# Stick-breaking attention in a hybrid decoder step: when the room of a pair's sample and meta key rows goes back to the arena

## The chip, the cores and the metric

The kernel runs on one core of one Trainium2 chip. The metric is the device time of one execution in microseconds (us); three timed runs of the kernel before gave 1514.38, 1515.96 and 1517.47 us, median 1515.96 us. One more execution was recorded by the profiler; every row of a trace below is from it.

The engines of a core are PE (matrix products, with PEld for its weight loads), DVE (elementwise work and scans), ACT (activations and copies), POOL (masks, memsets and gathers) and SP, which here only issues transfers. Each engine takes its instructions strictly in program order, and waits on counters (semaphores) that the other engines and the transfers raise.

## The reference

One layer of a decoder, with 512 prompt tokens behind 16 meta tokens, and 8 running sequences of 4 new tokens each with 256 cached positions. D_MODEL is 1024, and the attention has 16 heads of 64.

```python
def layer(x, s0, past_k, past_v, lead, ...):
    h = x + 0.5 * rms_norm(swiglu(rms_norm(x, ffn1_pre_g), ...), ffn1_post_g)
    proj = rms_norm(h, mix_pre_g) @ w_in
    q_a, k_a, v_a, gk_low, r_a, q_b, k_b, v_b, gate_a, gate_b = jnp.split(proj, offs, axis=-1)
    o_a, s_new = gla_branch(...)                      # gated linear attention, in chunks
    keys, vals = k_b, v_b                             # or the cached pages with k_b, v_b behind them
    o_b = sb_attend(q_b, keys, vals, sb_bias, q_off)  # stick-breaking attention
    m = sigmoid(gate_a) * (o_a @ w_o_gla) + sigmoid(gate_b) * (o_b @ w_o_sb)
    h = h + rms_norm(m @ w_out, mix_post_g)
    y = h + 0.5 * rms_norm(swiglu(rms_norm(h, ffn2_pre_g), ...), ffn2_post_g)
    return y, k_b, v_b, s_new

# sb_attend, for a query t and keys s < t:  z = q.k / 8 + bias
# A[t, s] = sigmoid(z_ts) * prod over s < j < t of (1 - sigmoid(z_tj))
```

The outputs that the change touches are the new key rows: `k_sample` (32 rows of the samples, output 5) and the first 16 rows of `k_prompt` (the meta tokens, output 2).

## The kernel before

The program is written out in order: PE, DVE, ACT and POOL execute what the code records, in the order in which it records it (`manual_schedule`). The main loops feed PE with matrix products of 128x128 weights in high and low halves (`tile_steps`, lines 681 to 684), and after each eighth of such a product, a **half step**, one call of `step()` runs the side work that has come due. `later(n, f)` puts a piece of side work n half steps ahead; `then(n, f)` puts it at half step n of the present pair.

**The attention** goes over 16 heads as 8 pairs, `Pair(0)` to `Pair(7)`, in a loop of nine passes of 24 half steps each. In a pass PE makes the queries, keys and values of the present pair (in the ninth pass, which has none, three gates instead) and the side work finishes the pair of the pass before. Of that side work these matter here:

- half step 6, `tails` (line 1735): PE transposes the pair's last 48 key columns (32 sample and 16 meta tokens; L1739), DVE copies them to `tk`, a room of 128 columns (L1745), and two transfers on SP's queue bring `tk` to the outputs: 16 KB of sample rows (L1747) and 8 KB of meta rows (L1748). Then `give(tk)`.
- half steps 9 to 14, `turned` (line 1755): three blocks of attention weights for each of the two heads are transposed by PE (L1763) and copied out of PSUM to a room `t` of 512 columns (L1766), by ACT for the first head and by DVE for the second.
- half step 14, `meta_turned` (PE L1788), and half step 17, `summed` (PE L1779, products with the values).

The passes of pairs 4 to 7 also work on the samples' cached pages: POOL issues gathers of 256 KB each (L1825), PE transposes the pages (L1874) and ACT copies them out. In the last pass these are eight gathers in a row.

**Rooms.** SBUF is one arena of 150 units of 280 columns in 25 chunks, `room0` to `room24`. `take(width)` finds units that are free in the recorded order, and prefers those that have been free for longest (`since`), after rules on evenness and on chunks still empty; `give` marks them free. Neither is an instruction. A room that is taken after it was given gets its new writer made to wait for what still reads or writes it, by waits that the framework adds. So `give` tells when a room may be found again, and a wait follows for whoever finds it while its old readers, here two transfers, have not ended. PSUM has two such rings of four buffers, `ps` and `acc`, that turn in the order of use.

Where the order of instructions is printed below, `room16_41_5215` is a chunk of the arena, `ps731` a PSUM buffer, and `DMAHW7_49` one of the eight counters on which SP's transfers are counted in turn; a transfer waits for the one before it on its own counter, so the names in SP's own rows tell on which it is counted.

Of the kernel before, what the change touches and what calls it, by code (L numbers as in the profile page):

```python
# [44 lines left out]
MIXER += [("S", "a", 4), ("R", "p", 2), ("R", "p", 3), ("S", "b", 4), ("S", "a", 6), ("R", "p", 4), ("R", "p", 5), ("S", "b", 6)]  # L45
MIXER += [("R", "p", 6), ("R", "p", 7)]
AHEAD = 150
SPREAD = 15
UNITS = 150


class Arena:
# [13 lines left out]
    def take(self, width, dt=F32, tight=False):  # L66
        k = -(-width // self.UNIT)
        best = None
        empties = sum(None not in f for f in self.freed)
        for c, free in enumerate(self.freed):  # L70
            empty = None not in free
            if not empty and self.tile[c].dtype != dt:
                continue
            for s in range(self.CHUNK - k + 1):
                f = free[s : s + k]
                if None in f:
                    continue
                since = max(f) if not empty else max(free) + SPREAD
                waste = k % 2 == 0 and s % 2
                alone = k == 1 and free[s ^ 1] is not None  # L80
                key = (empty and empties <= self.keep, waste, tight and sum(x is not None for x in free), alone, since)
                if best is None or key < best[0]:
                    best = (key, c, s)
        assert best is not None, f"no room for {width}: {[sum(x is not None for x in f) for f in self.freed]}"
        _, c, s = best
        if None not in self.freed[c] and (self.tile[c] is None or self.tile[c].dtype != dt):
            self.made += 1
            self.tile[c] = self.pool.tile([P, self.CHUNK * self.UNIT], dt, tag=f"room{c}", name=f"room{c}_{self.made}")
        self.freed[c][s : s + k] = [None] * k
        a = self.tile[c][:, s * self.UNIT : s * self.UNIT + width]  # L90
        self.held[id(a)] = (a, c, s, k)
        return a
# [9 lines left out]
    def give(self, *aps):  # L102
        for a in aps:
            _, c, s, k = self.held.pop(id(a))
            self.clock += 1
            self.freed[c][s : s + k] = [self.clock] * k
# [14 lines left out]
def hybrid_step(  # L121
# [16 lines left out]
    take, give = arena.take, arena.give  # L138
# [8 lines left out]
    def ps(tag="ps"):  # L147
        count[0] += 1
        return pp.tile([P, 512], F32, tag=tag, name=f"{tag}{count[0]}")
# [566 lines left out]
    def later(n, f):  # L716
        todo.append([n, f])
# [884 lines left out]
    class Pair:  # L1602
# [133 lines left out]
        def tails(self):  # L1736
            pr, kf, vf = self.pr, self.kf, self.vf
            p = ps()
            T.transpose(p[:NTL, :P], kf[:, :NTL], ident)  # L1739
            T.transpose(p[:NTL, P : 2 * P], vf[:, NP:], ident)  # L1740
            T.transpose(p[:, 2 * P : 3 * P], vfm[pr % 2], ident)
            fc = slice(P * (pr % 4), P * (pr % 4) + P)
            self.vm = vm = take(P)
            tk = take(P)
            V.tensor_copy(tk[:NTL], p[:NTL, :P])  # L1745
            c = slice(self.c0, self.c0 + P)
            nc.sync.dma_start(k_sample.rearrange("o b t h d -> (o b t) (h d)")[:, c], tk[:NS])  # L1747
            nc.sync.dma_start(kp_out[:NM, c], tk[NS:NTL])  # L1748
            give(tk)
            V.tensor_copy(tail_v[pr // 4][:NTL, fc], p[:NTL, P : 2 * P])  # L1750
            V.tensor_copy(vm, p[:, 2 * P : 3 * P])
            give(kf, vf)
# [700 lines left out]
```

## Time and profile before

| what | us |
|---|---|
| median of three timed runs | 1515.96 |
| the profiled execution, its own time | 1509.63 |
| span of its records | 1507.9 |
| PE busy in the span | 1495.4 (99%) |
| DVE busy | 1038.6 (69%) |
| ACT busy | 758.5 (50%) |
| POOL busy | 149.1 (10%) |

The span is the time from the first to the last record of the execution; 1.7 us of its own time lie around it. Busy times are sums over instructions; an engine that is busy 99% of the span is one for which nearly all the others' waits cost nothing, and only its own idle stretches can be taken out. The chain of waits is the work that ended last, followed back from the end; the table of waits says who stood still until whom. In a timeline row stand start, duration, engine, line, operation and the number of instructions merged; in brackets the idle time before the first of them and what ended it.

### The profile page before, as it was taken

What the parts mean: (1) busy time and instruction counts of PE and PEld (TensorE: products, weight loads), DVE (VectorE), ACT (ScalarE), POOL (GpSimd) and SP (SyncE); (2) the same over time, 40 slices, a digit from 0 to 9 for tenths busy, and PEclk for the clock granted to TensorE, in tenths of its full rate; (3) what the DMA queues carried; (4) which work ended last, traced back from release to release, by engine and by line L of the source; (5) the groups of instructions that cost most, each with busy time, mean ns of one, the idle gap of its engine ahead of it and who ended that gap; (6) DMA issues with size and microseconds to landing.
All of it is one profiled execution on the core that took longest, in us unless ns stands there. A gap on an engine that the chain in (4) does not pass through costs nothing.

```text
span 1507.9 us, 29580 instructions
## 1 busy us (share of the span) xinstructions
PE 1495.4 (99%) x11959; PEld 1444.0 (96%) x11959; DVE 1038.6 (69%) x1831; ACT 758.5 (50%) x1400; POOL 149.1 (10%) x216
## 2 busy tenths in 40 slices
PE   9999999999999999999999999999999999999998
PEld 8999999999999889899988999999999999999997
DVE  5888888523787857777776534977567888885234
ACT  6445454433665657565555443534564554544234
POOL 2000000000000111123224651000000000000000
PEclk9999999999999999999999999999999999999999
DMA  8123334524655473334455668434531343334343
GB/s 250 55 86 99 98 98 137 145 77 131 161 138 154 124 108 84 92 83 119 126 105 131 189 195 194 110 96 136 168 111 50 101 145 110 99 97 118 90 116 99
DMA packets 279561, 181.84 MB, mean 121 GB/s; under 512 B 10154, under 2 KB 264416, under 8 KB 279424
## 3 DMA queue, kind: packets, MB, share of 16 engines
q1 hardware_dynamic: 273968, 163.09, 41.0%
q0 software_dynamic: 5440, 16.85, 3.1%
q8 instruction: 94, 1.54, 0.4%
q14 instruction: 43, 0.35, 0.1%
q10 hardware_dynamic: 16, 0.00, 0.0%
HBM read 157.17 MB, written 22.74 MB: 119 GB/s over the span
## 4 chain that ended last, share of the span: by engine, by line
PE 95%; DVE 2%; DMA 1%; ACT 1%; issue 0%; SPq 0%; DVEq 0%; ACTq 0%
PE acc L694 10%; PE acc L697 10%; PE acc L695 10%; PE acc L681 8%; PE acc L1146 8%; PE acc L1144 8%; PE acc L1145 8%; PE acc L682 7%; PE acc L684 7%; PE acc L1087 2%; PE acc L1084 2%; PE acc L1085 2%; PE ps L1779 1%; PE acc L924 1%; PE acc L925 1%; PE acc L926 1%
## 5 line engine op out<-in xcount | busy, mean ns | idle before, releaser
L152 DVE TENSOR_TENSOR lo<-raw,hi 128x1024 fp32r<-128x1024 f32 (+1 forms) x216 | 258.6, 1198 | 174.8 <-ACT hi L660 166.3
L152 DVE TENSOR_TENSOR room<-room,room 128x544 fp32r<-128x544 f32 (+16 forms) x367 | 237.4, 669 | 122.4 <-ACT room L738 55.7
L681 PE MATMUL acc<-room,hi 128*128 128x280 f32 (+1 forms) x928 | 271.4, 309 | 0.1
L1146 PE MATMUL acc<-room,lo 128*128 128x280 f32 (+1 forms) x896 | 259.5, 290 | 0.0
L1145 PE MATMUL acc<-room,hi 128*128 128x280 f32 (+1 forms) x896 | 259.3, 289 | 0.0
L1144 PE MATMUL acc<-room,hi 128*128 128x280 f32 (+1 forms) x896 | 259.1, 289 | 0.0
L682 PE MATMUL acc<-room,hi 128*128 128x280 f32 (+1 forms) x928 | 250.5, 289 | 0.0
L694 PE MATMUL acc<-room,hi 128*128 128x280 f32 (+1 forms) x784 | 222.0, 292 | 0.0
L695 PE MATMUL acc<-room,hi 128*128 128x280 f32 (+1 forms) x784 | 219.0, 290 | 0.0
L660 ACT CAST hi<-raw 128x1024 fp32r<-128x1024 f32 (+1 forms) x130 | 131.9, 1015 | 145.0 <-PE acc L695 125.3
L684 PE MATMUL acc<-room,lo 128*128 128x280 f32 (+1 forms) x928 | 192.8, 289 | 0.0
L697 PE MATMUL acc<-room,lo 128*128 128x280 f32 (+1 forms) x784 | 192.3, 290 | 0.0
L681 PEld LDWEIGHTS acc<-room,hi 128*128 128x128 f32 x928 | 174.9, 188 | 13.0 <-issue 11.0
L682 PEld LDWEIGHTS acc<-room,hi 128*128 128x128 f32 x928 | 175.1, 189 | 2.8 <-issue 1.9
L1146 PEld LDWEIGHTS acc<-room,lo 128*128 128x128 f32 x896 | 168.6, 188 | 0.0
L1144 PEld LDWEIGHTS acc<-room,hi 128*128 128x128 f32 x896 | 168.6, 188 | 0.0
L1145 PEld LDWEIGHTS acc<-room,hi 128*128 128x128 f32 x896 | 168.4, 188 | 0.0
L694 PEld LDWEIGHTS acc<-room,hi 128*128 128x128 f32 x784 | 147.6, 188 | 2.0 <-issue 0.9
L695 PEld LDWEIGHTS acc<-room,hi 128*128 128x128 f32 x784 | 147.6, 188 | 0.2
L684 PEld LDWEIGHTS acc<-room,lo 128*128 128x128 f32 x928 | 145.0, 188 | 0.0
L855 ACT CAST hi<-raw 128x1024 fp32r<-128x1024 f32 x86 | 90.1, 1052 | 107.8 <-PE acc L1145 47.0
L697 PEld LDWEIGHTS acc<-room,lo 128*128 128x128 f32 x784 | 134.0, 188 | 0.0
(352 smaller groups left out, 2858.2 us busy)
## 6 DMA issues: line engine op xcount, KB each, us to landing
raw<-in_w_in_dram SPq DMA_DIRECT2D x49, 512.0 KB, 7.2
raw<-in_ffn_w_down_dram SPq DMA_DIRECT2D x42, 448.0 KB, 3.9
raw<-in_ffn_w_gate_dram SPq DMA_DIRECT2D x64, 256.0 KB, 3.3
raw<-in_ffn_w_up_dram SPq DMA_DIRECT2D x64, 256.0 KB, 3.3
raw<-in_ffn_w_down_dram SPq DMA_DIRECT2D x21, 512.0 KB, 4.0
out_dram<-room SPq DMA_DIRECT2D x32, 256.0 KB, 3.1
raw<-in_w_in_dram SPq DMA_DIRECT2D x28, 256.0 KB, 4.3
h_dram<-room SPq DMA_DIRECT2D x24, 280.0 KB, 3.1
```

What stands on the lines that cost most here:

```text
L152: (eng or V).tensor_tensor(out=out, in0=a, in1=b, op=op)
L660: S.copy(h_, src)
L681: T.matmul(acc[h][:, : wid[h]], hi[k], a[h][0], start=(k == 0), stop=False)
L682: T.matmul(acc[h][:, : wid[h]], hi[k], a[h][1], start=False, stop=False)
L684: T.matmul(acc[h][:, : wid[h]], lo[k], a[h][0], start=False, stop=(k == KD - 1))
L694: T.matmul(acc[h][:nw, : wid[h]], wh, a[h][0], start=(k == 0), stop=False)
L695: T.matmul(acc[h][:nw, : wid[h]], wh, a[h][1], start=False, stop=False)
L697: T.matmul(acc[h][:nw, : wid[h]], wl, a[h][0], start=False, stop=(k == kt - 1))
L855: S.copy(hi[:, :kt], src)
L1144: T.matmul(x[:, :QW], hi, act[k][0], start=(first and k == 0), stop=False, skip_group_check=True)
L1145: T.matmul(x[:, :QW], hi, act[k][1], start=False, stop=False, skip_group_check=True)
L1146: T.matmul(x[:, :QW], lo, act[k][0], start=False, stop=(k == 3), skip_group_check=True)
```

## The change

In `tails`, the room `tk` is no longer given back in the half step that issues its two transfers, but by `later(LEAVE, ...)` twelve half steps later, at half step 18 of the pass instead of 6.

```diff
 AHEAD = 150
+LEAVE = 12
 SPREAD = 15
@@ class Pair, tails
             nc.sync.dma_start(k_sample.rearrange("o b t h d -> (o b t) (h d)")[:, c], tk[:NS])
             nc.sync.dma_start(kp_out[:NM, c], tk[NS:NTL])
-            give(tk)
+            later(LEAVE, lambda: give(tk))
             V.tensor_copy(tail_v[pr // 4][:NTL, fc], p[:NTL, P : 2 * P])
```

No instruction is added, dropped or moved on any engine. What changes is which rooms later takers find, and with them some waits: the rooms of `tk`, of `vm` (the meta values, L1751), of `am` (the meta weights, L1713) and of a few scratch rows in the attention, and from there on chunks 12 and 22 in exchanged parts. A line more at the top makes every line number behind it one higher in the changed kernel.

DVE in the last pass, where pair 7's tails are copied; before:

```order
L1745 COPY room16_41_5215<-ps727_9212 48x128 [waits DMAHW7_49,DMAHW0_49,PE_49]
L1750 COPY room23_39_5177<-ps727_9212 48x128
L1751 COPY room12_46_5436<-ps727_9212 128x128
L1701 SCALAR_TENSOR_TENSOR room16_41_5215<-room16_41_5215,room5_6_71 128x16 [waits DVE_49]
L152 TENSOR_TENSOR room11_45_5365<-room11_45_5365,room16_41_5215 128x831 [waits DVE_49,Pool_49]
```

and now:

```order
L1746 COPY room4_5_70<-ps727_9212 48x128 [waits PE_49]
L1751 COPY room23_39_5177<-ps727_9212 48x128
L1752 COPY room11_45_5365<-ps727_9212 128x128
L1702 SCALAR_TENSOR_TENSOR room16_41_5215<-room16_41_5215,room5_6_71 128x16 [waits DVE_49]
L153 TENSOR_TENSOR room11_45_5365<-room11_45_5365,room16_41_5215 128x831 [waits DVE_49,Pool_49]
```

`tk` of pair 7 moves from chunk 16, where each pair since pair 3 had found the unit of the pair before it, to chunk 4; the copy no longer waits for pair 6's transfers (the two counters).

ACT a few half steps later, at the first head's three copies out of PSUM; before:

```order
L1766 COPY room22_33_983<-ps730_9255 128x512 [waits PE_49]
L1766 COPY room16_41_5215<-ps731_9275 128x384 [waits DMAHW0_49,DVE_49,DMAHW7_49,PE_49,Activation_49]
L660 CAST hi732_9290<-raw699_8922 128x1024 [waits DMAHW1_49]
L1766 COPY room5_6_71<-ps734_9296 128x384 [waits DVE_49,PE_49,Activation_49]
L2026 CAST room2_48_6208<-room14_35_3119 128x544 [waits DVE_49]
```

and now:

```order
L1767 COPY room22_33_983<-ps730_9255 128x512 [waits PE_49]
L1767 COPY room16_41_5215<-ps731_9275 128x384 [waits DVE_49,PE_49,Activation_49]
L661 CAST hi732_9290<-raw699_8922 128x1024 [waits DMAHW1_49]
L1767 COPY room5_6_71<-ps734_9296 128x384 [waits DVE_49,PE_49,Activation_49]
L2027 CAST room2_48_6208<-room14_35_3119 128x544 [waits DVE_49]
```

The second copy takes the same two units of chunk 16 in both programs. Before, one of them was the unit that `tk` had given back four half steps earlier, and the copy waits for the two transfers on `DMAHW7` and `DMAHW0`, which are pair 7's own (SP's rows L1747 and L1748 of that pair stand on those counters); now these two waits are gone.

DVE where pair 4's first head is weighed (half step 2 of the pass of pair 5); before:

```order
L152 TENSOR_TENSOR room12_46_5436<-room12_46_5436,room16_41_5215 128x831 [waits DVE_49,Pool_49]
L152 TENSOR_TENSOR room12_46_5436<-room12_46_5436,room5_6_71 128x1
L152 TENSOR_TENSOR room12_46_5436<-room12_46_5436,room5_6_71 128x511 [waits Pool_49]
L1713 COPY room3_4_69<-room12_46_5436 128x16 [waits DVE_49]
L1713 COPY room3_4_69<-room12_46_5436 128x16 x2
```

and now:

```order
L153 TENSOR_TENSOR room12_46_5436<-room12_46_5436,room16_41_5215 128x831 [waits DVE_49,Pool_49]
L153 TENSOR_TENSOR room12_46_5436<-room12_46_5436,room5_6_71 128x1
L153 TENSOR_TENSOR room12_46_5436<-room12_46_5436,room5_6_71 128x511 [waits Pool_49]
L1714 COPY room12_46_5436<-room12_46_5436 128x16 [waits DMAHW6_49,DMAHW5_49,DVE_49]
L1714 COPY room12_46_5436<-room12_46_5436 128x16 x2
```

`am` of pair 4 moves to the unit in chunk 12 that held pair 2's `tk`, and its first copy now waits for pair 2's transfers. The `am` of pairs 5, 6 and 7 wait in the same way for those of pairs 3, 4 and 5, and pair 2's `tk` copy (L1745) for those of pair 1, a wait that before stood two instructions behind it. The mask rows of the samples on POOL (L1835) wait for pair 0's, and a memset of POOL (L1910) and two copies of ACT (L1876) and two of DVE behind the last pass for transfers of pair 6 and older ones.

## The prediction

> **What bounds the kernel now.** I read the busy table first, then the chain of waits, then the table of waits, and after that the timelines of the one place that these point at.
>
> ```profile
> span 1507.9 us, 29580 instructions
> ...
> PE 1495.4 (99%) x11959; PEld 1444.0 (96%) x11959; DVE 1038.6 (69%) x1831; ACT 758.5 (50%) x1400; POOL 149.1 (10%) x216
> ...
> PE 95%; DVE 2%; DMA 1%; ACT 1%; issue 0%; SPq 0%; DVEq 0%; ACTq 0%
> ```
>
> PE is busy for 1495.4 of 1507.9 us, so all its idle time together is 12.5 us. The change adds and drops no instruction; it can gain only what of these 12.5 us hangs on a wait that it takes away, and lose only by a new wait that reaches PE. In the chain one per cent, some 15 us, is transfers. The table of waits says where PE stands, and what ACT has to do with it:
>
> ```profile
> ACT room L1766 <- DMA out_dram<-room: 7.0, 1, 7.0
> ...
> PE ps L2388 <- DVE room L152: 3.2, 1, 3.2
> PE ps L1763 <- ACT room L1766: 2.3, 1, 2.3
> PE acc L1238 <- DVE own L255: 1.1, 1, 1.1
> PE ps L2388 <- ACT room L2389: 0.7, 1, 0.7
> PE ps L1788 <- ACT room L1766: 0.7, 1, 0.7
> ```
>
> Two of PE's waits lie at the end of the program (L2388) and one at its start (L1238). The other two, 2.3 and 0.7 us, are for the copies of L1766, and ACT itself stood 7.0 us before one such copy, for a transfer to an output. That is the place of this change, once, in pair 7. ACT's timeline and the chain in that window:
>
> ```profile
> 810.42 0.59 ACT L1766 COPY room<-ps 128x512 f32<-128x512 f32 x1 [0.62 <-PE ps L1763]
> 818.02 0.48 ACT L1766 COPY room<-ps 128x384 f32<-128x384 f32 x1 [7.01 <-DMA out_dram<-room]
> 818.39 1.05 ACT L660 CAST hi<-raw 128x1024 fp32r<-128x1024 f32 x1
> 819.34 0.48 ACT L1766 COPY room<-ps 128x384 f32<-128x384 f32 x1
> ...
> 809.07 0.15 SPq L1747
> 809.28 8.56 DMA out_dram<-room
> ```
>
> The second copy stands from 811.0 to 818.02 us: its room holds the unit that `tk` gave back at half step 6, and the 8 KB of meta rows that are read out of it, issued at 809.28, land 8.56 us later, at 817.84.
>
> **What the wait costs PE.** The same products in pair 6, where nothing waits, against pair 7 (PE's timeline; the first four rows are pair 6):
>
> ```profile
> 783.62 0.49 PE L1763 MATMUL ps<-ident,room 128*128 128x128 f32 x3
> 784.72 0.49 PE L1763 MATMUL ps<-ident,room 128*128 128x128 f32 x3
> 785.05 0.27 PE L1788 MATMUL ps<-ident,room 128*128 128x128 f32 x1
> 787.56 1.73 PE L1779 MATMUL ps<-room,room 128*64 128x512 f32 x8
> ...
> 811.74 0.49 PE L1763 MATMUL ps<-ident,room 128*128 128x128 f32 x3
> ...
> 815.10 0.49 PE L1763 MATMUL ps<-ident,room 128*128 128x128 f32 x3
> 818.64 0.52 PE L1763 MATMUL ps<-ident,room 128*128 128x128 f32 x3 [2.29 <-ACT room L1766]
> 819.88 0.33 PE L1788 MATMUL ps<-ident,room 128*128 128x128 f32 x1 [0.72 <-ACT room L1766]
> 822.38 2.37 PE L1779 MATMUL ps<-room,room 128*64 128x512 f32 x16
> ```
>
> Between the last two groups of transposes lie 784.72 - 783.62 = 1.10 us in pair 6 and 818.64 - 815.10 = 3.54 us in pair 7: 2.44 us lost. From there to L1788 it is 0.33 against 1.24 us: 0.91 us lost, since the third copy stands behind the late second one and a cast of 1.05 us on ACT. From L1788 to L1779 it is 2.51 against 2.50: nothing more. The PSUM ring of four buffers is what ties PE to ACT: the last group of transposes needs the buffer of the copy that waits. **The price is 2.44 + 0.91 = 3.35 us**; the idle times in brackets sum to 3.0, less, because a matmul's modelled end lies behind the next one's start.
>
> **The change part by part.** *The wait that goes.* ACT's second copy then waits for its transposes (811.74 + 0.49 = 812.23 us) and for DVE's weighing, done by then; it starts about 5.8 us earlier, with the cast and the third copy behind it, at some 812.2, 812.6 and 813.6 us. PE wants the buffer at 815.10 + 1.10 = 816.2 and the third copy's at 816.5, so 3 us and more are to spare, and the whole 3.35 us come back. DVE's second-head copies, the weights' low half and SP's next weight transfer, all behind that cast, move up with it. What would be late next: nothing in this pass that pairs 4 to 6 do not do without a wait. Behind it every term of PE's idle time is the start or the end of the program, so what is won here is kept.
>
> *The waits that move.* These are the added ones on DVE, ACT and POOL in the part on the change. Their transfers are old when they are waited for. The nearest is pair 2's `tk` copy behind pair 1's transfers:
>
> ```profile
> 656.14 0.26 DVE L1745 COPY room<-ps 48x128 f32<-48x128 f32 x1
> ...
> 627.02 0.33 SPq L1747 DMA_DIRECT2D out_dram<-room  x1
> ...
> DMA to landing us min/median/max: 3.0/6.5/10.2
> ```
>
> 29 us lie between issue and use, and no transfer of L1747 took over 10.2 us. The `am` copies wait for transfers of two pairs back, twice that. On DVE there stand scans and PE's next blocks behind them, so cover that failed would cost PE what it overshoots; that needs a landing nearly three times the longest. I take 0.
>
> *The unit that is held.* Twelve half steps more, from half step 6 to 18. Half steps 6 and 17 of pair 6's pass:
>
> ```profile
> 775.62 0.27 PE L1739 MATMUL ps<-ident,room 128*48 128x128 f32 x1
> ```
>
> From there to L1779 at 787.56 are eleven half steps in 11.9 us, so twelve are 13 us: longer than the longest landing of 10.2 us, so whoever takes the unit at 18 or later finds the transfers over. One unit of 150 less, in those half steps, makes takers choose other rooms; it adds no instruction. I take 0.
>
> *What is unknown* is how late the transfers land in a run that isn't profiled. Pair 4, which also has gathers beside it, and pair 7, each with its issue of L1747 and the landing:
>
> ```profile
> L1747 SPq DMA_DIRECT2D out_dram<-room x1: 333/333/333, 714.1 to 714.1; - x1
> DMA to landing us min/median/max: 6.5/6.5/6.5
> ...
> L1747 SPq DMA_DIRECT2D out_dram<-room x1: 337/337/337, 808.9 to 808.9; - x1
> DMA to landing us min/median/max: 8.1/8.1/8.1
> ```
>
> Each us of landing is one us of PE's wait until it is gone. With pair 4's 6.5 us instead of 8.1 the price is 3.35 - 1.6 = 1.75; with the longest of the eight, 10.2, it is 5.45; with the shortest, 3.0, it is nothing. In pair 7 the transfers run beside the heaviest traffic of the attention:
>
> ```profile
> 804.00:812.00 8.00, 8.00 (x73) 6.82 (x71) 7.82 (x19) 2.93 (x6) 5.96 (x5) 1.00 0.84 105
> 812.00:820.00 8.00, 4.99 (x42) 4.56 (x39) 2.07 (x5) 1.98 (x4) 5.26 (x7) 1.00 0.84 279
> ...
> raw<-in_w_in_dram SPq DMA_DIRECT2D x1, 512.0 KB, 10.8
> room<-in_cache_k_dram,idx POOLq DMA_INDIRECT x4, 10.5
> ```
>
> The first two rows are windows (last columns: PE clock, the transfer engines' busy share, GB/s): the engines are 84% busy in both. The other two are transfers issued in the same 16 us: the weights' take 10.8 us and the key gathers 10.5, as late as the 8 KB. The traffic is the program's own and comes in every run, so I take the profile's 8.1 us and the range 1.75 to 5.45 around it. [...]
>
> **The sum.** Profiled execution 1509.63 - 3.35 = 1506.28 us, span 1504.55. The timed runs are 1515.96 - 1509.63 = 6.33 us longer than the profiled one, for reasons that no row shows; they do the same work, so I take the term over: 1515.96 - 3.35 = **1512.6 us**, 0.22% faster. I call faster or slower what differs by over 0.2%, 3.03 us, about what a measurement of this kernel can tell from no change; the forecast lies just beyond that bound.
>
> **The rivals.** *A longer stall in the timed runs.* They are all 4.8 to 7.8 us longer than the profiled run, PE's work is the same, and what can vary is transfers. If pair 7's landed at 11 us, as the weights' beside them did (10.8), the price is 3.35 + 2.7 = 6.05 us, 1509.9 us. Against it: some of the difference may lie anywhere else. On PE's clock the trace shows no loss after the gap, 1.00 granted in the row of 812 to 820 us. [...]
>
> *No change, since the transfers land sooner without the profiler.* At 4.7 us of landing (8.1 - 3.35) or less, nothing is left: 1516.0 us. For it: the shortest of the eight pairs took 3.0; against it: pair 4, beside gathers too, took 6.5.
>
> *Slower: the weight transfer that moves up delays the key pages.* SP's next 512 KB are issued at 820.73 us, behind the late cast; now they go out near 815, into the gathers' traffic, and the pages feed PE's transposes:
>
> ```profile
> 820.73 0.40 SPq L185 DMA_DIRECT2D raw<-in_w_in_dram  x1
> ...
> 809.61 1.75 POOL L1825 DMA_INDIRECT room<-in_cache_k_dram,idx x1 [0.30 <-issue]
> ...
> 832.88 0.60 PE L1874 MATMUL ps<-ident,room 128*128 128x128 f32 x4
> ```
>
> The last key gather lands at 809.61 + 10.5 = 820.1 us, and PE wants it at 832.88 - 3.35 = 829.5: 9.4 us of slack. 512 KB at the slower window's 105 GB/s are 5.0 us, so the pages would still be there. From 9.4 us of delay on it decides, and each us more costs one; at 16 us it would be 6.6 - 3.35 = 3.2 us slower, 1519.2 us. I see nothing that makes it so long.
>
> **How the numbers follow.** Forecast, a stall of 1.75 to 5.45 us gone: 0.72, two thirds of it (0.50) beyond 3.03 us, since its middle is 3.35 and the profiled run is the shortest of the four. A longer stall: 0.14, all beyond. No change: 0.08. Slower: 0.06, by that mechanism or one like it. Faster is 0.50 + 0.14 = 0.64, the same 0.22 + 0.08 = 0.30, slower 0.06. The likeliest case's own range is 1510.5 to 1514.2; for 8 in 10 I take the longer stall's 1509.4 at the low end and 1515.6 at the high one, where little of the stall is gone.
>
> **What would show it.** In the changed kernel's profile: no wait of ACT's L1767 for a transfer; the last group of L1764 1.10 us behind the one before it, and L1789 0.33 us behind that; PE's idle time at 9 to 9.5 us instead of 12.5, in a span near 1504.5. The next weight transfer (L186) leaves near 815 us. A new wait of PE, DVE or ACT for an `out_dram` transfer would make the part on moved waits wrong; a stall that is gone in the profile with a median that has not moved would make the last step, from the profiled execution to the timed runs, wrong.

## The result and the profile after

| kernel | median | runs | |
|---|---|---|---|
| before | 1516.02 us | 10, 1514.38 to 1517.85 | |
| changed | 1511.49 us | 10, 1511.14 to 1513.76 | ratio 0.9975, 95% interval 0.9966 to 0.9985 |

The change saves 4.5 us, 0.25%; the forecast was 1512.6 us and 0.22%. In the changed kernel each line number behind the new constant is one higher (L1766 is L1767 now). Its busy table and its chain of waits:

```profile
span 1509.4 us, 29576 instructions
...
PE 1496.7 (99%) x11959; PEld 1444.4 (96%) x11959; DVE 1038.9 (69%) x1831; ACT 758.3 (50%) x1400; POOL 150.6 (10%) x216
...
PE 96%; DVE 1%; ACT 1%; issue 1%; DMA 1%; ACTq 0%; DVEq 0%; SPq 0%
```

This span is longer than the 1507.9 us of the profile before, though the kernel is faster. The two executions differ in something else, and the table of waits shows in what (columns: total us, times, longest). The count of records falls by four (29580 before), but those that count for the engines are the same in both profiles: 11959, 1831, 1400 and 216.

```profile
PE ps L2389 <- DVE room L153: 3.2, 1, 3.2
PE ps L1975 <- issue: 2.8, 5, 0.8
PE acc L1239 <- DVE own L256: 1.1, 1, 1.1
```

The waits of L1764 and L1789 for ACT are gone. A new one stands at L1975, the products with the value pages, 23 us and more behind the place of the change; it waits for nothing that the profile shows. The experiments say below where it belongs. At the place of the change, ACT's, PE's and SP's timelines read now:

```profile
810.09 0.59 ACT L1767 COPY room<-ps 128x512 f32<-128x512 f32 x1 [0.62 <-PE ps L1764]
811.98 0.48 ACT L1767 COPY room<-ps 128x384 f32<-128x384 f32 x1 [1.30 <-PE ps L1764]
812.36 1.05 ACT L661 CAST hi<-raw 128x1024 fp32r<-128x1024 f32 x1
813.30 0.48 ACT L1767 COPY room<-ps 128x384 f32<-128x384 f32 x1
```

```profile
814.77 0.49 PE L1764 MATMUL ps<-ident,room 128*128 128x128 f32 x3
815.86 0.49 PE L1764 MATMUL ps<-ident,room 128*128 128x128 f32 x3
816.18 0.27 PE L1789 MATMUL ps<-ident,room 128*128 128x128 f32 x1
```

```profile
814.69 0.40 SPq L186 DMA_DIRECT2D raw<-in_w_in_dram  x1
```

The second copy starts at 811.98 us, right behind its transposes, and not at 818.02. The last group of transposes stands 1.09 us behind the one before it (3.54 before), L1789 0.32 behind that (1.24 before). The next weight transfer left at 814.69.

### The profile page after: what moved, and what is told of

The parts are those of the page before. It is cut to its first block, busy times and chain, and to the rows that moved or that the text cites. A ratio compares the mean times of both kernels' runs of the same rounds, so it can differ in the third digit from the quotient of the medians.

```text
span 1509.4 us, 29576 instructions
## 1 busy us (share of the span) xinstructions
PE 1496.7 (99%) x11959; PEld 1444.4 (96%) x11959; DVE 1038.9 (69%) x1831; ACT 758.3 (50%) x1400; POOL 150.6 (10%) x216
## 4 chain that ended last, share of the span: by engine, by line
PE 96%; DVE 1%; ACT 1%; issue 1%; DMA 1%; ACTq 0%; DVEq 0%; SPq 0%
PE acc L695 10%; PE acc L698 10%; PE acc L696 10%; PE acc L682 8%; PE acc L683 8%; PE acc L1147 8%; PE acc L1146 8%; PE acc L1145 8%; PE acc L685 8%; PE acc L1088 2%; PE acc L1085 2%; PE acc L1086 2%; PE ps L1780 1%; PE acc L925 1%; PE acc L926 1%; PE acc L927 1%
## 5 line engine op out<-in xcount | busy, mean ns | idle before, releaser
L682 PEld LDWEIGHTS acc<-room,hi 128*128 128x128 f32 x928 | 174.8, 188 | 13.0 <-issue 10.8
```

The lines of the kernel that those rows point to most:

```text
L682: T.matmul(acc[h][:, : wid[h]], hi[k], a[h][0], start=(k == 0), stop=False)
```

## The experiments

Kernels of one group ran on one chip, with their own runs of the kernel before. Medians of that kernel differ between chips: 1511.24 us for the first group, 1511.32 for the second, 1515.21 for the third, 1516.02 in the result. A comparison is therefore made within a group.

### Both kernels again, on one chip

The kernel before and the changed one, without an edit. The question was whether the pauses at L1975 are the change's.

> The kernel before, unchanged, to get a second profile of it, since its first one (1509.63 us) is 4.75 us shorter than the fastest of ten timed runs (1514.38). Theory A (the wait is the whole change): ratio to before 1.000; ACT's second copy of L1766 in pair 7 stands 6 to 9 us for a transfer, PE loses 3 to 4.5 us there. If in addition the products with the value pages (L1974) stand for some 5 us, as the changed kernel's do (4.9 us over four places) and the first profile of before did not, then those waits are a thing of most runs of both kernels and no price of the change. Theory B (the change buys 3.35 us at pair 7 and pays 4.9 us of them back at the value pages): no such stall at L1974 here, and the 4.75 us lie somewhere else.

> The changed kernel, unchanged, beside the others on one chip. Theory A: 0.997 to 0.998 of before, no wait of ACT or PE for a transfer in pair 7, and the idle time at the value pages (L1975) of the same size as in the kernel before's second profile. Theory B: the idle time at L1975 is 4 to 5 us here and under 1 us in the kernel before.

The kernel before took 1511.56 us (11 runs, 1509.67 to 1513.27; 1.0003 of the group's other runs of it, 0.9994 to 1.0012), the changed one 1506.57 (6 runs, 1506.02 to 1507.65; ratio 0.9970, 0.9958 to 0.9982). PE's timeline of the kernel before, then the span and the same rows of the changed one:

```profile
815.25 0.49 PE L1763 MATMUL ps<-ident,room 128*128 128x128 f32 x3
818.88 0.52 PE L1763 MATMUL ps<-ident,room 128*128 128x128 f32 x3 [2.38 <-ACT room L1766]
820.11 0.33 PE L1788 MATMUL ps<-ident,room 128*128 128x128 f32 x1 [0.72 <-ACT room L1766]
```

```profile
span 1504.3 us, 29576 instructions
```

```profile
814.81 0.49 PE L1764 MATMUL ps<-ident,room 128*128 128x128 f32 x3
815.90 0.49 PE L1764 MATMUL ps<-ident,room 128*128 128x128 f32 x3
816.23 0.27 PE L1789 MATMUL ps<-ident,room 128*128 128x128 f32 x1
```

From the last undisturbed group of transposes to the product of L1788 the kernel before takes 820.11 - 815.25 = 4.86 us, the changed one 816.23 - 814.81 = 1.42: 3.44 us. The predicted term was 3.35. The span is 1504.3 us, where 1504.55 was forecast, and PE's idle time in it 1504.3 - 1494.6 = 9.7 us, where 9 to 9.5 was. Neither trace has a pause at the value products, so the change does not bring them; whether the chip does was still open after this group.

### Which of the moved waits counts

In the changed kernel, the room is held longer in the last pair alone:

```diff
-            later(LEAVE, lambda: give(tk))
+            later(LEAVE, lambda: give(tk)) if pr == 7 else give(tk)
```

> The delay of twelve half steps for the last pair's room alone; the rooms of pairs 0 to 6 go back at once, as before. Theory A (one wait, in the last pass, is all that the change is worth): the whole gain, 0.997 to 0.998 of before, no wait of ACT's copies for a transfer at pair 7 and PE's last two groups of transposes 1.10 us apart. Rival (the held rooms of the earlier passes, or the room numbers that move with them, bring part of the gain): less than half of it, 0.999 or more.

1506.24 us (6 runs, 1506.14 to 1506.65; ratio 0.9965, 0.9953 to 0.9977), as the changed kernel within its scatter. The gain comes from pair 7 alone; held rooms and moved waits of the other seven pairs cost and bring nothing that can be told.

### The transfers two half steps later

The kernel before, with pair 7's two transfers and the return of their room put into a function that is called two half steps later:

```diff
-            nc.sync.dma_start(k_sample.rearrange("o b t h d -> (o b t) (h d)")[:, c], tk[:NS])
-            nc.sync.dma_start(kp_out[:NM, c], tk[NS:NTL])
-            give(tk)
+            def send():
+                nc.sync.dma_start(k_sample.rearrange("o b t h d -> (o b t) (h d)")[:, c], tk[:NS])
+                nc.sync.dma_start(kp_out[:NM, c], tk[NS:NTL])
+                give(tk)
+
+            later(2, send) if pr == 7 else send()
```

> The kernel before, but pair 7's two transfers are issued, and its room is given back, two half steps later (half step 8); the copies find the same rooms as before. Theory A, one us of landing is one us of PE's wait: two half steps are 2.1 us, so ACT stands about 9 us instead of 7, PE loses 5 to 6 us instead of 3.35, 1.5 to 2.5 us slower than before, 1.0010 to 1.0017. Rival (the landing is set by the traffic around it and ends at the same time whenever the transfers are issued): ACT's wait ends at the same time as in the kernel before, and the ratio is 1.000.

1511.77 us (11 runs, 1509.59 to 1513.56; ratio 1.0001, 0.9992 to 1.0010). The edit delayed nothing: SP is not among the engines whose order is written out by half steps, and it issued both transfers as soon as `tk` was copied, the first at 809.1 us, where the group's unedited kernel has 809.0. So this run tells nothing about a longer stall. Its trace shows something else. Stretches of 4 us in the trace of the kernel before and of this one (columns: busy time of PE, of its weight loads, of DVE, ACT and POOL, then the granted clock, the transfers' share, GB/s):

```profile
816.00:820.00 4.00, 1.02 (x8) 0.59 (x6) 0.29 (x1) 1.75 (x4) 2.23 (x4) 1.00 0.68 254
820.00:824.00 4.00, 3.89 (x27) 2.99 (x29) 3.96 (x9) 1.29 (x4) 0.00 (x0) 1.00 0.21 59
```

```profile
816.00:820.00 4.00, 1.29 (x8) 0.81 (x6) 0.00 (x0) 1.39 (x3) 2.23 (x4) 0.81 0.72 254
820.00:824.00 4.00, 3.64 (x17) 3.53 (x17) 3.90 (x8) 1.48 (x5) 0.00 (x0) 0.50 0.16 48
824.00:828.00 4.00, 4.00 (x25) 2.45 (x25) 2.05 (x5) 0.17 (x1) 0.00 (x0) 0.84 0.30 93
```

Behind nearly the same gap PE's clock is granted at half here, from 818.5 us (half speed for 1.5 of the first 4 us makes 0.81) to 825.3, and at 1.00 throughout in the kernel before. There 27 matmuls start from 820 to 824 us, here 17. What that costs can be read from two products in the two timelines, the kernel before first (in this kernel lines behind the edit are 4 higher):

```profile
825.80 1.02 PE L1795 MATMUL ps<-room,room 128*128 128x512 f32 x2
```

```profile
819.24 0.88 PE L1767 MATMUL ps<-ident,room 128*128 128x128 f32 x3 [2.71 <-ACT room L1770]
...
828.26 1.02 PE L1799 MATMUL ps<-room,room 128*128 128x512 f32 x2
```

At the end of the gap it is 819.24 - 818.88 = 0.36 us behind, at the second product 828.26 - 825.80 = 2.46: the halved clock cost 2.1 us, on top of the wait.

### The transfers sent twice

The kernel before and the changed one, with pair 7's two transfers issued a second time behind the first (the same rows to the same place):

```diff
-            nc.sync.dma_start(k_sample.rearrange("o b t h d -> (o b t) (h d)")[:, c], tk[:NS])
-            nc.sync.dma_start(kp_out[:NM, c], tk[NS:NTL])
+            for _ in range(2 if pr == 7 else 1):
+                nc.sync.dma_start(k_sample.rearrange("o b t h d -> (o b t) (h d)")[:, c], tk[:NS])
+                nc.sync.dma_start(kp_out[:NM, c], tk[NS:NTL])
```

> The kernel before, with pair 7's two transfers issued twice (the second time behind the landing of the first), so that the room is free some 3 us later; the result stays the same. Theory A, one us of landing is one us of PE: ACT stands about 10 us instead of 7.1, PE loses 3 us more between its last groups of transposes. In addition, if PE's clock is what makes the kernel before scatter from 1509.7 to 1514.3 us: the gap is then over 5 us long, the clock is granted at 0.5 for one or two windows of 3.4 us behind it in every run, 1.7 to 3.4 us more. Together 3 to 6.4 us slower than the median of before, 1.002 to 1.004. Rival (PE has other work to do meanwhile, and the wait is hidden by what is queued): 1.000.

> The same double transfers in the changed kernel, whose copies do not wait for them. Theory A: no wait of ACT or PE for them, the time of the changed kernel, 0.997 of before, within 0.001. Rival (the extra transfers cost by themselves): as much slower than the changed kernel as the run before this one is slower than the kernel before.

With the room returned at once, 1514.80 us (11 runs, 1514.36 to 1515.91; ratio 1.0023, 1.0014 to 1.0032); with the room held, 1506.42 (5 runs, 1505.83 to 1506.60; ratio 0.9962, 0.9948 to 0.9975). So the transfers themselves cost nothing that can be told, and the wait for their room, with what the clock does behind it, is all. The waits and a stretch of the slower one:

```profile
ACT room L1767 <- DMA out_dram<-room: 11.1, 1, 11.1
...
PE ps L1764 <- ACT room L1767: 6.4, 1, 6.4
```

```profile
820.00:824.00 4.00, 0.87 (x3) 0.50 (x3) 0.16 (x1) 1.62 (x3) 0.00 (x0) 0.50 0.04 16
```

ACT waits 11.1 us instead of the 7.1 of the first group's kernel before, and PE 6.4 at this place instead of 2.4: 4.0 us more on each, so here one us of landing is one us of PE. The clock is halved here too.

### What makes the landing late: the gathers behind

The kernel before and the changed one, with the four value gathers of half step 10 of the last pass asked for at half step 23:

```diff
-                then(10, ask)
...
                 then(23, ask)
+                then(23, ask)
```

> The kernel before, but the last pass's four gathers of value pages stand behind the memsets of its half step 22 on POOL instead of right behind the four of key pages, so that pair 7's transfers have half the gathers beside them, as in pairs 4 to 6. If the traffic makes them land late (8.1 us, 9.0 after the second's issue): they land in 6 to 7 us, ACT's wait falls from 7.1 to 5 us or less and PE's loss from 3.4 to 1.5 us or less; 1 to 3 us faster at that place. What it can cost is a wait of the products with these pages (L1974), which come 9 us behind the gathers. Rival (the landing is long for another reason, such as SP's slow issue): ACT's wait stays at 7 us.

> The same later value gathers in the changed kernel. Theory A (the traffic matters at pair 7 through the wait alone): nothing to win at pair 7, the time of the changed kernel within 0.001, or slower by what the products with the value pages then wait. Rival (less traffic helps elsewhere too): as much faster than the changed kernel as the run before this one is faster than the kernel before.

1511.52 us (11 runs, 1508.87 to 1512.59; ratio 0.9997, 0.9988 to 1.0006) with the room returned at once, 1506.51 (5 runs, 1505.98 to 1506.64; ratio 0.9962, 0.9948 to 0.9975) with it held. The wait and three stretches of the first, then two of PE's rows:

```profile
ACT room L1766 <- DMA out_dram<-room: 7.7, 1, 7.7
```

```profile
816.00:820.00 4.00, 0.65 (x5) 0.31 (x3) 0.08 (x1) 1.54 (x3) 0.00 (x0) 1.00 0.10 34
820.00:824.00 4.00, 3.68 (x18) 3.68 (x19) 3.97 (x8) 1.51 (x4) 0.00 (x0) 0.59 0.15 43
824.00:828.00 4.00, 4.00 (x28) 2.37 (x27) 1.91 (x5) 0.00 (x0) 0.00 (x0) 0.98 0.29 88
```

```profile
819.09 0.52 PE L1763 MATMUL ps<-ident,room 128*128 128x128 f32 x3 [2.96 <-ACT room L1766]
...
827.51 1.02 PE L1795 MATMUL ps<-room,room 128*128 128x512 f32 x2
```

The transfer engines are 10% busy from 816 to 820 us instead of 68%, and the wait is as long as before: 7.7 us. What is issued behind the small transfers did not set their landing here, though I had expected it to. Here, too, the clock is halved behind the gap, for one stretch of 3.4 us (0.59 and 0.98 of two windows of 4 us), which begins at about 820.7 us, when PE had been at work again since 819.09. Against the kernel before of the first group (818.88 and 825.80 us) this run is 0.21 us behind at the first of the two products and 1.71 at the second: 1.5 us lost behind the gap.

### What makes the landing late: the gathers and weights ahead

The kernel before, first with both sets of gathers at half step 23, then with the weight fetch of half step 3 at half step 7, then with both edits:

```diff
-                then(6, ask)
-                then(10, ask)
...
+                then(23, ask)
+                then(23, ask)
```

```diff
-                then(n, st.fetch)
+                then(7 if pr == 8 and n == 3 else n, st.fetch)
```

> The kernel before, with the key gathers of the last pass (four of 64 KB or more, issued from 804.6 to 809.8 us, ahead of the tail transfers) and the value gathers moved to half step 23 of that pass, so that no gather is issued between 800 and 818 us; only the 512 KB of weights (issued at 805.5) are still ahead of the two tail transfers. Theory A (what is issued ahead sets the landing, and the gathers are the larger part of it): the meta rows land 3 to 5 us after their issue instead of 8.6, ACT's second copy waits 0 to 3.5 us instead of 7.1, PE at most 0.5 for it. Theory B (the weights alone set it): landing 7 to 8.6, ACT waits 6 to 7.1 and PE 2 to 3 as before. The time says little here: the key pages come late, PE may wait up to some us for them behind 829 us.

> The kernel before, with the 512 KB weight transfer of half step 3 of the last pass put behind the two tail transfers in SP's order (half step 7); the gathers stay where they are. Theory B (the weights ahead set the landing): the meta rows land 3 to 5 us after their issue, ACT waits 0 to 3.5 us, PE at most 0.5, and the median comes 3 to 4.7 us under before's unless the weights, which then land some 6 us later, are missed by the cast of half step 11. Theory A (the gathers): landing 7 to 8.6, ACT waits 6 to 7.1, PE 2 to 3, median as before within 2 us.

> Both edits of the two runs before it: gathers at half step 23 and the weight transfer behind the tail transfers. Traffic ahead, whichever kind: landing 3.0 to 4 us, the shortest of the eight pairs being 3.0; ACT waits under 2.5 us and PE not at all for it. If the landing stays at 7 us or more with nothing ahead, traffic is not the cause, and the transfer's own form (8 KB in small pieces, SP's 2.0 us of issue) or the write to the output is.

The weight edit did not do what it says: SP issued its transfers in the same order, the weights at 805.36 us, ahead of the small ones. So the second kernel behaves as the kernel before once more (1515.52 us, 10 runs; ratio 0.9998, 0.9988 to 1.0007), and the third as the first once more. Theory B, the weights alone, was tested all the same, since both have the weights ahead and no gathers. ACT's timeline of the first, then SP's and ACT's of the third:

```profile
813.07 0.48 ACT L1766 COPY room<-ps 128x384 f32<-128x384 f32 x1 [1.81 <-DVE room L152]
```

```profile
804.94 0.46 SPq L185 DMA_DIRECT2D raw<-in_w_in_dram  x1
808.50 0.34 SPq L1747 DMA_DIRECT2D out_dram<-room  x1
808.89 0.41 SPq L1748 DMA_DIRECT2D out_dram<-room  x1
```

```profile
812.31 0.48 ACT L1766 COPY room<-ps 128x384 f32<-128x384 f32 x1 [1.70 <-DMA out_dram<-room]
```

In the third, the transfer issued at 808.89 is the last that ACT waits for, and ACT goes on at 812.31: 3.4 us after the issue instead of 8.7 to 9.4 in the traces with the key gathers there, with the weights still ahead. In the first ACT waits for DVE, and for no transfer. SP's issue of L1748 takes 0.41 us in pair 7 instead of 2.0 to 3.1, so 1.6 to 2.7 of the 5.3 to 6.0 us lie within the issue. These kernels move the value gathers too, but those alone changed nothing in the runs above: the key gathers make the landing late, and theory B falls. By which of their steps they do it is open. Both kernels are slower as wholes, 1521.73 us (5 runs; ratio 1.0039, 1.0025 to 1.0054) and 1522.40 (4 runs; 1.0045, 1.0028 to 1.0061). PE then waits for the key pages, 4.9 and 5.1 us; the mean granted clock of the two traced executions is 0.995 and 0.997. What the wait and the clock make of the loss was not added up.

The second kernel answers the question that the first group had left, for its group's chip is one of the longer medians. PE's timeline of the value products in it, and the same products in the first group's kernel before:

```profile
843.23 0.50 PE L1974 MATMUL ps<-room,room 128*32 128x128 f32 x6
844.18 0.43 PE L1974 MATMUL ps<-room,room 128*32 128x128 f32 x4 [0.45 <-issue]
844.89 0.27 PE L1974 MATMUL ps<-room,room 128*32 128x128 f32 x1 [0.28 <-issue]
845.61 0.87 PE L1974 MATMUL ps<-room,room 128*32 128x128 f32 x21 [0.45 <-issue]
```

```profile
843.03 1.06 PE L1974 MATMUL ps<-room,room 128*32 128x128 f32 x32
```

The 32 products go through in one stretch there, and are broken up by pauses here, in a kernel that does the same in the same order. The spans are 1512.9 and 1508.0 us. The pauses were in all three traces of this group's chip and in the changed kernel's first profile, and in none of the eight of the first two groups. The first profile of the kernel before has none either, although its ten timed runs are of the longer kind; its 1509.63 us lie below all of them (1514.38 at least), and the record does not say on which chip it or the result was taken. So the pauses do not come with the change. They go with the chip as far as these three chips show, and why one has them is not shown.

The same trace has a wait at L1763 as long as the one with the halved clock above, and the clock at 1.00 behind it:

```profile
PE ps L1763 <- ACT room L1766: 2.7, 1, 2.7
```

```profile
820.00:824.00 4.00, 3.68 (x25) 2.85 (x27) 3.97 (x8) 1.50 (x4) 0.00 (x0) 1.00 0.18 56
```

## Why the prediction was right, and where it was off

**The place and the price.** Right. The one wait removed is that of pair 7's second copy; it was put at 3.35 us and measures 3.44 between two traces of one chip. The same difference of rows makes 3.8 us in two other traces, where ACT waited 7.4 us instead of 7.0 to 7.1. Holding the room in the last pair alone gives the whole gain.

**The moved waits and the held unit, both at nothing.** Right: the changed kernel's tables of waits have none of PE, ACT's copies or DVE for an `out_dram` transfer, POOL's stand at lines that had them before, within 0.6 us as long, and pair 7 alone is as good as all eight.

**The sum from the profiled execution.** The span of 1504.55 us was met at 1504.3. The first profiles could not show it: one has the pauses at the value products and the other has not.

**"The timed runs are ... 6.33 us longer than the profiled one, for reasons that no row shows."** Taking the term over was right, and most of it probably has a row now: the pauses at L1974. Two traces of the same program's work, with them and without, differ by 1512.9 - 1508.0 = 4.9 us of span, and the changed kernel's first profile has them too. A trace of the kernel before on the chip of the result, which would settle it, is not there.

**The size in the timed runs.** This term was too small. The forecast of 1512.6 us came out 1.1 us too long. The median gains 4.5 us in the result and 1511.24 - 1506.57 = 4.7 in the first group, some 1.1 to 1.3 more than the 3.4 of the wait. The step that missed it: "On PE's clock the trace shows no loss after the gap". That is one execution's answer, and the row cited for it ends at 820 us, while in the run of the value gathers the halving begins only at about 820.7. Of the six traces that have the wait, three (the kernel before twice, and the second of the third group) show the clock at 1.00 behind it, and three show it halved for one or two stretches of 3.4 us, at 1.5 us for one stretch and 2.1 for two in the runs of the value gathers and of the later transfers.

The runs agree with it: 33 of the 34 of the kernel before in the first group scatter over 3.6 us (1509.67 to 1513.27, and one at 1514.26), six of the changed one over 1.6 (1506.02 to 1507.65); the quickest differ by 3.65 us, and the medians by 4.67. The record also holds the mean granted clock of each of these runs. The six of the kernel before at 0.999 have a median of 1509.88 us, the ten at 0.996 one of 1512.54; the changed kernel's two at 0.999 took 1506.53 and 1506.62. At the same high clock the change is thus worth 3.3 us, the wait alone, and the runs with a lower clock are the longer ones. The mean counts halved stretches anywhere (in the first profiles of both kernels they lie in the last 8 us, 0.76 and 0.73 granted from 1500 to 1508 us), and a lower mean is not always a longer run: with the room held in the last pair alone, three runs at 0.997 took 1506.15 to 1506.27 us, and the one at 0.999 took 1506.14. (The run of 1514.26 stands at 0.946, and is of another kind.) There is no trace of each timed run, so how much of the median's gain is the clock is not measured run by run.

The rival of a longer stall was partly true, mostly by the halved clock, 1.5 and 2.1 us behind two such waits: the wait for a later landing varied too, but less, 2.3 to 2.7 us of PE between the four traces that change nothing ahead of or behind the transfers.

What brings the clock down is not shown. Behind a wait of 2.7 us in one run (the later transfers) it was granted at 0.50 from 818.5 us, about 2 us after PE had stopped (819.24 - 2.71 = 816.53), and behind one of 2.7 us in another (the second of the third group) at 1.00 from 816 to 824 us.

**A slip in the range.** Its low end is called the longer stall's 1509.4 us, but that rival's own sum gives 1509.9. The measured 1511.49 lies above both, so nothing hangs on it.

**What makes the landing late.** "The traffic is the program's own and comes in every run" held, but the row of 84% busy engines does not carry it: the wait stayed when the later half of that traffic was taken away. It is the four key gathers, issued from 804.6 us on, ahead of the small transfers and beside them. With the weights alone ahead ACT goes on 3.4 us after the issue. Without the gathers the weights, issued at 804.94 us, land 6.7 us later, at 811.64, and ACT goes on behind the small transfer at 812.31; with them, in the first profile of the kernel before, the weights took 10.8 us. No run here shows by what the gathers delay them.

**The slower rival.** The weight transfer did move up, to 814.69 us, and PE's table of waits has no row for the key pages: the slack held. It was a little larger than the 9.4 us of the sum, which took the median of the four gathers, 10.5 us; the last one landed in 9.3.

## What to carry to other kernels

A room that a small output transfer still reads is not free when the transfer is issued (8 KB landed 8.56 us later here, and ACT stood 7.0 us for it): return it by the longest landing that the traffic ahead can make, and look for its wait where the last pass differs from the others. A stall of PE of 2 to 4 us can be worth more in the median than in a profile that shows the clock at 1.00 behind it (4.67 us against 3.44 here), so read several runs' scatter beside the one trace. And before a new wait in a profile is put down to a change, the unchanged kernel has to be seen on the same chip.

## What was not expected of the hardware

- Behind waits of PE of 3.0, 2.7 and 6.4 us the clock was granted at 0.50 for 3.4 to 6.8 us, 1.5 and 2.1 us lost behind the first two; behind waits of 2.3 to 2.7 us in three other traces it was not. In one run the halved stretch began 1.6 us after PE had resumed.
- A product stream without any wait (L1974, 32 small matmuls) stops for 0.3 to 1.0 us several times in all three traces of one chip and in none of the eight of two others, some 4.3 us of PE time over four such streams in the second kernel of the third group (its lag behind the first group's kernel before grows from 0.2 us at L1763 to 4.55 at the last broken product). Why is open; it was not tried.
- SP's issue of pair 7's 8 KB transfer took 2.0 to 3.1 us with the key gathers under way, 0.41 without. Gathers are not all that lengthens it: in the first profile the same line took 2.04 us in pair 0, which has no gathers, and 0.67 in pair 5, which has. SP issued when the data were there, and half steps did not hold it: with the call two half steps later the first of pair 7's transfers left at 809.1 us, without it at 809.0.
